# 28 column blocks of an input projection as seven products over both sequences, with other projections between the heads

## The chip, the cores and the metric

The kernel runs on one core of a Trainium2 chip. The metric is the device time of one execution in microseconds (us), as a median of several. TensorE (PE) multiplies matrices, VectorE (DVE), ScalarE (ACT) and GpSimd (POOL) do the elementwise work, and SyncE (SP) issues most of the DMAs.

## The reference

One encoder layer on two sequences of 512 tokens with 1024 channels in float32: a half-step feed-forward block, a mixing block, a second half-step feed-forward block and a last norm.

```
def encoder_layer(x, ...):
    x = x + 0.5 * swiglu(rms_norm(x, ffn1_norm), ffn1_w_gate, ffn1_w_up, ffn1_w_down)
    h = rms_norm(x, mix_norm)
    proj = h @ w_in                                    # 1024 x 4880
    aq, ak, av, mq, mk, mv, gate_pre, o_pre, g_att, g_mlstm = jnp.split(proj, split_at, axis=-1)
    aq = apply_rope(rms_norm(aq.reshape(B, S, 8, 64), q_norm), cos, sin)
    ak = apply_rope(rms_norm(ak.reshape(B, S, 2, 64), k_norm), cos, sin)
    att = gqa_block_attention(aq, ak, av)              # 8 heads of 64, 2 key/value heads
    mem = mlstm_bidirectional(mq, mk, mv, gate_pre, mlstm_gate_bias, o_pre, mlstm_head_norm)   # 4 heads of 128
    merged = jax.nn.sigmoid(g_att) * (att @ w_up_att) + jax.nn.sigmoid(g_mlstm) * (mem @ w_up_mlstm)
    x = x + merged @ w_out
    return x + 0.5 * swiglu(rms_norm(x, ffn2_norm), ffn2_w_gate, ffn2_w_up, ffn2_w_down)
```

In the memory heads each of the two directions needs running maxima of a gate value over the tokens, by which its exponentials are scaled.

## The kernel before

Activations lie with channels on the partitions and 512 tokens along the free axis. A float32 product is made of three matmuls: both operands are split into a high and a low part (`split`, line 658; weights: line 240; one on ACT for the high part, one on DVE for the low), and hi·hi, hi·lo and lo·hi are summed in PSUM.

Five stages follow each other: feed-forward 1 up (0 to 447 us of the span), down (447 to 656), mixing of both sequences (656 to 1431), feed-forward 2 up (1431 to 1854) and down (1854 to 2063), then a tail. In the up stage (class `Up`, matmuls of `product`, line 333) a two by two block product of weights (two column blocks) with tokens (two sequences, two halves of the channels) is made of seven products of sums instead of eight: for each pair of column blocks `gu_left_a/b/c` build and split the sums of weights, and `right_sums` builds those of the tokens once (tiles `xc[B11]`, `xc[B21]`, `xc[B22]`, `xc[T1..T4]`). For ten pairs the first two products, which need sequence 0 alone, are made ahead (`begin`), while the other token sums are still being built; their results wait in DRAM (`kept`).

The mixing stage is a generator `mix(s, ...)`, run for sequence 0 and then 1, the two interleaved at its `yield`s. `tok_proj` (line 739) makes keys, values and gates (272 columns in all), queries (512) and memory values (512) with tokens on the partitions. The other 28 blocks of 128 columns go through `proj_w` (line 755), 24 matmuls of 128x512 each, per sequence: 8 attention gates (`att_gate`), 8 memory gates (`mem_gate`), 4 output gates (`out_gate`), 4 memory queries and 4 memory keys (`mem_qk`). Sequence 0 loads and splits the weights and parks both parts in DRAM (`load_w`, `parked`); sequence 1 loads the parts. These blocks stand in a `queue`, out of which `fill(n)` takes n units after each head, so that PE has something to do while DVE, ACT and POOL work for the head:

```
for h in range(HA):                       # 8 attention heads
    nxt = scores(h + 1) if h + 1 < HA else None
    attend(h, Ps)                         # row maxima, exp, scale, split, transposes, P.V
    ...
    fill(1 if h < 4 else 2)
```

An attention head is: scores (line 1001, 8 matmuls), row maxima (DVE, 1004), exp (ACT, 1006), reciprocal and scaling (1007, 1008), 16 transposes (1020) with a split (658), and P·V (1028, 8 matmuls; drained in 1036 and 1037). Before the heads come the ropes (`rope_apply`, lines 796 to 807), with mean squares (785) and inverse roots in small DVE steps (`rstd_cols`, lines 162 to 192), and transposes to head layout (keys 847, queries 941). A memory head (`mem_head`, `mem_out`) is: scores (1117), exponentials (ACT, 1131), products (1133), merged directions (1144, 1145), transposes (1159) and products with the values (1167); its maxima come out of `mem_max` (POOL add and two DVE reduces, 967 to 973, for each head and direction) and `mem_scales`. `merge_att` and `merge_mem` multiply by the output projections of the two branches and the gates; `out_unit` is one block of the last projection, which for sequence 0 lies around the ropes and heads of sequence 1.

The order of the instructions on each engine is set when the kernel is built: a scheduler takes them by priority, which is the order in the program, moved by `shifted(n)`. On the chip each engine runs its own list in order, and waits for semaphores. Tiles come out of pools with few buffers, so a new tile can wait until an old one was read for the last time.

Of the kernel before, what the change touches and what calls it, by code (L numbers as in the profile page):

```python
# [8 lines left out]
F32 = mybir.dt.float32  # L9
# [7 lines left out]
P = 128  # L17
# [9 lines left out]
def encoder(ctx, tc, I, outs):  # L27
# [679 lines left out]

    held = []

# [12 lines left out]
    def tok_proj(xh, xl, cols, kk, done):  # L722
# [7 lines left out]
        def comp(k0, w):  # L730
            wh, wl = w
            if not p:
                p.extend([MM(), MM(), MM(), PO()])
            for kl in range(kk):
                k = k0 + kl
                for b in range(4):
                    bs = slice(b * P, (b + 1) * P)
                    for i, (a, w_) in enumerate(((xh, wh), (xh, wl), (xl, wh))):
                        nc.tensor.matmul(p[b][:, :N], a[:, k, bs], w_[:, kl, :],  # L739
                                         start=(k == 0 and i == 0), stop=(k == KD - 1 and i == 2))  # L740
            if k0 + kk == KD:
                done(p)

        return [(lambda k0=k0: load(k0), lambda w, k0=k0: comp(k0, w)) for k0 in range(0, KD, kk)]

# [12 lines left out]
    OUT = 3  # L758

    def mix(s, xh, xl, early=None, extra=None, after=None):  # L760

        xsrc = lambda k: (xh[:, k, :], xl[:, k, :])
        queue = []

        def fill(n):
            go(*queue[:n])
            del queue[:n]
# [3 lines left out]

        def win_cols(c0, done):
            return proj(win_v[:, :, c0:c0 + P], ("in", c0), xsrc, KD, done)

# [5 lines left out]
        Gt = small(64, "gt")  # L780
# [32 lines left out]
        def kv_done(pk):  # L813
            for b in range(4):
# [6 lines left out]
                                        op0=ALU.mult, op1=ALU.subtract)  # L821
            ssk = small(8, "ssk")
# [10 lines left out]
        def q_done(pq):  # L833
            ssq = small(32, "ssq")
            for b in range(4):
                t = T2()
                nc.scalar.activation(t, pq[b], AF.Copy, scale=r[s][:, b:b + 1])
# [20 lines left out]
        ebuf = dpool.tile([2, 4, S], F32, name=nm("ebuf"))  # L858

        def gates():  # L860
            Gb = Gt.rearrange("p (b c) -> p b c", b=4)
# [24 lines left out]
            for d in range(2):  # L886
                p = PT()
                for b in range(4):
                    nc.tensor.transpose(p[0:4, b * P:(b + 1) * P], ev[:, d, b, :], ident)
                er = F2()  # L890
                V_.tensor_copy(er[0:4], p[0:4])
                nc.sync.dma_start(ebuf[d], er[0:4])


        Vm = []

        def mem_values():
            def done(pvv):
                vm = A([P, 2, 4, S], F32R, "Vm")
                for b in range(4):  # L900
                    nc.scalar.activation(vm[:, 0, b, :], pvv[b], AF.Copy, scale=r[s][:, b:b + 1])
                    V_.scalar_tensor_tensor(vm[:, 1, b, :], pvv[b], r[s][:, b:b + 1], f(vm[:, 0, b, :]),
                                            op0=ALU.mult, op1=ALU.subtract)
                Vm.append(vm)
            return tok_proj(xh, xl, [(1792, 512)], 2, done)
# [3 lines left out]
        def mem_qk(h, j):  # L909
            def done(pp):  # L910
                if j == 0 and not s:
                    t = wpool.tile([P, 4, S], F32R, tag="w8", bufs=4, name=nm("qk"))
                    qks[h] = [t[:, i] for i in range(4)]
                elif s:
                    t = wpool.tile([P, 2, S], F32R, tag="wr", bufs=4, name=nm("qk"))
                    qks.setdefault(h, []).extend(t[:, i] for i in range(2))
                t = F2()
                V_.tensor_tensor(t, pp, R[s], op=ALU.mult)
                split(t, *qks[h][2 * j:2 * j + 2])
            return win_cols((768, 1280)[j] + h * P, done)  # L920
# [3 lines left out]
        def out_gate(h):  # L924
            def done(pp):
                og = T2(F32, "ac")
                V_.tensor_tensor(og, pp, R[s], op=ALU.mult)
                nc.scalar.activation(og, og, AF.Tanh, scale=0.5)
                G_.tensor_scalar(og, og, 1.0, hn[:, h:h + 1], op0=ALU.add, op1=ALU.mult)
                ogs[h] = og  # L930
            return win_cols(2320 + h * P, done)
# [13 lines left out]
        go(*tok_proj(xh, xl, [(512, 256), (2304, 16)], 2, kv_done))  # L945
        if early:
            early()
        go(*tok_proj(xh, xl, [(0, 512)], 2, q_done), mem_qk(0, 0))
        yield None
# [5 lines left out]
        go(mem_qk(0, 1), mem_qk(1, 0), mem_qk(1, 1))  # L955

        st = spool.tile([P, 4, 2, 4, HM], F32, tag="st", bufs=1, name=nm("st"))
        n1, bd, en, n2 = [st[:, i] for i in range(4)]

        def mem_rows(h, d):  # L960

            eb = T2(F32, "eb")
            nc.sync.dma_start(eb, ebuf[d, h:h + 1, :].rearrange("a s -> (a s)").partition_broadcast(P))
            em = T2(F32, "eb")
            eb3 = eb.rearrange("p (b s) -> p b s", b=4)
# [3 lines left out]

        def mem_max(h, d):  # L970
            eb3, em3 = mem_rows(h, d)
            V_.tensor_reduce(n1[:, d, :, h], em3, axis=AX.X, op=ALU.max)
# [549 lines left out]
```

## Time and profile before

| what | us |
|---|---|
| median of 3 runs (lowest, highest) | 2085.64 (2085.07, 2087.56) |
| the profiled execution's own time | 2083.45 |
| its span | 2081.4 |
| PE, DVE, ACT, POOL busy | 2060.3, 1573.6, 895.4, 111.2 |
| mean granted PE clock | 0.999 |

The profile is one execution. Times in it are from the start of the span. Engines are listed with their busy time; for a group of instructions the page gives line, engine, operation, tiles out<-in, shape and count, then the busy time, the mean duration of one in ns and the idle time of the engine before them with what ended it. The chain is followed back from the last instruction: each piece has its start, its length, and the engine, tile and line.

### The profile page before, as it was taken

The numbers are of one execution on the slowest core, as the hardware profiler recorded it, in microseconds if no ns is written. First come the engines' busy times: TensorE is split into PE (matmuls) and PEld (weight loads), VectorE is DVE, ScalarE is ACT, GpSimd is POOL, SyncE is SP. The second block draws the span as 40 slices with busy tenths as digits, with TensorE's granted clock in tenths as the row PEclk, the third lists the DMA queues.
The fourth block names the chain that finished last, engine by engine and source line by source line (L and its number), as shares of the span: only waits on it lengthen the run. The fifth ranks groups of instructions, "written<-read, shape, count | busy, mean of one in ns | idle before, by whom it ended". The sixth has DMA issues, their size and how long they took to land.

```text
span 2081.4 us, 27314 instructions
## 1 busy us (share of the span) xinstructions
PE 2060.3 (99%) x9488; PEld 1694.0 (81%) x9488; DVE 1573.6 (76%) x2870; ACT 895.4 (43%) x1645; POOL 111.2 (5%) x122
## 2 busy tenths in 40 slices
PE   8999999999999999999999999999999999999998
PEld 6888888888888877888887788888888888888887
DVE  7888888786797899575568846555788888785797
ACT  6544444443234566463344543324444444442222
POOL 1000000001003012100120000002000000000010
PEclk9999999999999999999999999999999999999999
DMA  8656555699766655777685345677656555599753
GB/s 277 208 171 195 193 171 182 201 346 359 260 223 243 216 167 198 257 240 272 214 283 193 112 153 188 208 258 244 200 177 201 193 172 182 187 339 350 273 189 117
DMA packets 303161, 458.52 MB, mean 220 GB/s; under 512 B 20304, under 2 KB 170848, under 8 KB 302000
## 3 DMA queue, kind: packets, MB, share of 16 engines
q1 hardware_dynamic: 301152, 451.32, 64.4%
q0 software_dynamic: 1872, 5.46, 0.8%
q8 instruction: 75, 1.23, 0.2%
q14 instruction: 62, 0.51, 0.1%
HBM read 289.82 MB, written 166.89 MB: 219 GB/s over the span
## 4 chain that ended last, share of the span: by engine, by line
PE 92%; DVE 3%; DMA 3%; ACT 1%; issue 1%; SPq 0%; POOL 0%; DVEq 0%; ACTq 0%; POOLq 0%
PE mm L755 19%; PE pss L333 17%; PE pst L333 11%; PE mm L333 10%; PE mm L589 9%; PE pst L589 4%; PE pss L589 4%; PE mm L739 4%; PE pso L589 3%; PE pso L739 1%; PE pso L1028 1%; PE pso L1167 1%; PE pst L755 1%; PE pss L755 1%; PE pss L1117 1%; PE pst L1020 1%
## 5 line engine op out<-in xcount | busy, mean ns | idle before, releaser
L755 PE MATMUL mm<-xh,w 128*128 128x512 f32 x896 | 290.6, 394 | 0.0
L333 PE MATMUL pss<-xc,w 128*128 128x512 f32 x1056 | 256.4, 392 | 0.2 <-DVE t L364 0.2
L333 PE MATMUL mm<-xc,w 128*128 128x512 f32 x1056 | 253.5, 391 | 2.2 <-ACT w L291 1.4
L333 PE MATMUL pst<-xc,w 128*128 128x512 f32 x1056 | 253.8, 390 | 0.1
L333 PEld LDWEIGHTS pss<-xc,w 128*128 128x128 f32 x1056 | 197.0, 188 | 47.4 <-DVE t L364 6.7
L333 PEld LDWEIGHTS mm<-xc,w 128*128 128x128 f32 x1056 | 197.4, 188 | 45.2 <-ACT w L291 2.3
L333 PEld LDWEIGHTS pst<-xc,w 128*128 128x128 f32 x1056 | 198.2, 188 | 41.6 <-ACT t L368 0.5
L755 PEld LDWEIGHTS mm<-xh,w 128*128 128x128 f32 x896 | 167.4, 188 | 33.6
L589 PE MATMUL mm<-rt,w 128*128 128x512 f32 (+1 forms) x819 | 188.4, 385 | 0.0
L755 PE MATMUL mm<-xl,w 128*128 128x512 f32 x448 | 176.0, 393 | 0.0
L589 PEld LDWEIGHTS mm<-rt,w 128*128 128x128 f32 x819 | 151.4, 188 | 29.8
L291 ACT ACTIVATE w<-t 128x512 fp32r<-128x512 f32 x176 | 106.9, 627 | 138.6 <-issue 55.2
L292 DVE TENSOR_TENSOR w<-t,w 128x512 fp32r<-128x512 f32 x176 | 118.3, 689 | 55.1 <-ACT w L291 53.1
L333 PE MATMUL pss<-xc,f 128*128 128x512 f32 x528 | 126.9, 389 | 0.0
L333 PEld LDWEIGHTS pss<-xc,f 128*128 128x128 f32 x528 | 99.1, 188 | 20.6
L657 ACT ACTIVATE w<-wr 128x512 fp32r<-128x512 f32 x72 | 45.1, 632 | 138.6 <-PE pso L589 70.8
L657 ACT ACTIVATE w<-t 128x512 fp32r<-128x512 f32 x82 | 51.8, 632 | 107.6 <-PE pst L589 62.4
L755 PEld LDWEIGHTS mm<-xl,w 128*128 128x128 f32 x448 | 84.3, 188 | 16.7
L589 PE MATMUL pst<-rt,w 128*128 128x512 f32 x396 | 93.7, 389 | 0.0
L589 PE MATMUL pss<-rt,w 128*128 128x512 f32 x396 | 93.7, 389 | 0.0
L589 PEld LDWEIGHTS pst<-rt,w 128*128 128x128 f32 x396 | 74.3, 188 | 15.4
L589 PEld LDWEIGHTS pss<-rt,w 128*128 128x128 f32 x396 | 74.3, 188 | 15.4
(337 smaller groups left out, 3666.9 us busy)
## 6 DMA issues: line engine op xcount, KB each, us to landing
rt<-rbuf SPq DMA_DIRECT2D x154, 512.0 KB, 5.5
wpark<-w SPq DMA_DIRECT2D x104, 512.0 KB, 3.6
w<-wpark SPq DMA_DIRECT2D x104, 512.0 KB, 4.8
wr<-in_ffn_w_gate_dram SPq DMA_DIRECT2D x62, 512.0 KB, 5.3
rbuf<-tab SPq DMA_DIRECT2D x102, 256.0 KB, 3.8
wr<-in_ffn_w_up_dram SPq DMA_DIRECT2D x44, 512.0 KB, 4.7
rbuf<-f SPq DMA_DIRECT2D x72, 256.0 KB, 3.7
wr<-in_w_in_dram SPq DMA_DIRECT2D x36, 512.0 KB, 5.7
```

The costliest lines, as they stand in the source:

```text
L291: pin(nc.scalar.activation(t[:, 0], src, AF.Copy))
L292: pin(V_.tensor_tensor(t[:, 1], src, f(t[:, 0]), op=ALU.subtract))
L333: nc.tensor.matmul(p, a[:, k, :], xt[:, b, k, :], start=(first and k == 0 and i == 0), stop=(k == HK_ - 1 and i == 2), skip_group_check=True)
L589: nc.tensor.matmul(p, u[:, a, d * P:(d + 1) * P], r[:, b, ts], start=(first and q == 0 and k == 0), stop=(q == len(us) - 1 and k == 2), sk ...
L657: nc.scalar.activation(hi, src, AF.Copy)
L739: nc.tensor.matmul(p[b][:, :N], a[:, k, bs], w_[:, kl, :], start=(k == 0 and i == 0), stop=(k == KD - 1 and i == 2))
L755: nc.tensor.matmul(p, a[:, k, :], b, start=(k == 0 and i == 0), stop=(k == n - 1 and i == 2))
L1020: nc.tensor.transpose(p[:, b * P:(b + 1) * P], Ps[b][:, kb * P:(kb + 1) * P], ident)
L1028: nc.tensor.matmul(po, Vst[:, kv_, hk, :], w, start=(kv_ == 0 and i == 0), stop=(kv_ == 3 and i == 1))
L1117: nc.tensor.matmul(p, qk[a][:, isl], qk[b], start=(n == 0), stop=(n == 2))
L1167: nc.tensor.matmul(po, vm[:, a, t, hs_], b, start=(t == 0 and n == 0), stop=(t == 3 and n == 2))
```

## The change

A new class `Joint` makes the 28 blocks for both sequences at once, as 14 pairs with seven products each, in a stage of its own between feed-forward 1 down and the mixing. Ten pairs are begun ahead with sequence 0's products. Results of gates are passed through tanh, those of memory queries and keys split, and all are stored in DRAM (`jbuf`); `mix` loads them where it needs them. Keys and gates of sequence 1 are made right after sequence 0's projections and parked (`kvpark`); queries and values of sequence 1 are made in halves of 256 columns (`tok_half`) and stand in the queue as fillers for the heads of sequence 0 (`FILLS[0]`); six of the eight output units of sequence 0 are the fillers for the heads of sequence 1 (`FILLS[1]`). The running maxima come from two `tensor_tensor_scan` on a 32x128 tile with the heads on the partitions and two transposes, in place of `mem_max`. The factor `hn` moves from POOL into a product on DVE.

```
+    JP = [(2832 + d * P, 3856 + d * P) for d in range(KD)]
+    JP += [(2320 + 2 * i * P, 2320 + (2 * i + 1) * P) for i in range(2)]
+    JP += [(768 + h * P, 1280 + h * P) for h in range(4)]
+    NJ, RAW, JAHEAD, JLAST = 14, 10, 10, 4
...
+    class Joint:
...
+        def out(self, s, j, u, t):
+            to = jbuf[s][j][u]
+            if j >= RAW:
+                hi = self.ring("h")
+                split(t, hi.bitcast(F32R), t.bitcast(F32R))
+                nc.sync.dma_start(to[:, 0], hi)
+                nc.sync.dma_start(to[:, 1], t)
+            else:
+                nc.scalar.activation(t, t, AF.Tanh, scale=0.5)
+                nc.sync.dma_start(to, t)
+        def first_a(self, W, t):
+            X = MM()
+            product(X, W[B11], self.xc[B11], True)
+            with shifted(SOONER):
+                V_.tensor_tensor(t, X, R[0], op=ALU.mult)
+            return X
...
+        def block(self, j, W, v1, mid):
+            ring, xc = self.ring, self.xc
+            Y, Z = PS(), PT()
+            second = lambda: product(Y, W[T2_], xc[T2_], True)
+            if v1 is not None:
+                second()
+            else:
+                v1 = ring("v")
+                X = self.first_a(W, v1)
+                second()
+                self.first_b(X, W, j, ring("h"))
...
+            product(Z, W[T1], xc[T1], True)
...
+            product(Y, W[T3], xc[T3], False)
...
+            product(Z, W[B22], xc[B22], False)
...
+            product(Y, W[T4], xc[T4], False)
...
+    def tok_half(src, col, half, done):
...
+                for b in range(4):
+                    bs = slice(b * P, (b + 1) * P)
+                    for i, (a, w_) in enumerate(((xh, wh), (xh, wl), (xl, wh))):
+                        nc.tensor.matmul(p[b // 2][:, (b % 2) * HW:(b % 2 + 1) * HW], a[:, bs], w_[:, kl, :], ...)
...
+    FILLS = ((0, 1, 1, 1, 1, 1, 0, 1, 2, 0, 0, 0), (0, 1, 0, 1, 0, 1, 0, 0, 1, 1, 1, 0))
...
-            for d in range(2):
-                p = PT()
-                for b in range(4):
-                    nc.tensor.transpose(p[0:4, b * P:(b + 1) * P], ev[:, d, b, :], ident)
-                er = F2()
-                V_.tensor_copy(er[0:4], p[0:4])
-                nc.sync.dma_start(ebuf[d], er[0:4])
+            p = PT()
+            nc.tensor.transpose(p[0:32, 0:P], et, ident)
+            rows = F2()[0:32]
+            er, run = rows[:, 0:P], rows[:, P:2 * P]
+            V_.tensor_copy(er, p[0:32, 0:P])
+            nc.sync.dma_start(ebuf.rearrange("d b h s -> (d b h) s"), er)
+            V_.tensor_tensor_scan(run[:, ::-1], er[:, ::-1], er[:, ::-1], NEG, op0=ALU.max, op1=ALU.max)
+            V_.tensor_tensor_scan(run[0:16], er[0:16], er[0:16], NEG, op0=ALU.max, op1=ALU.max)
...
-            if h >= 4:
-                mem_max(h - 4, 0)
-                mem_max(h - 4, 1)
-            fill(1 if h < 4 else 2)
+            fill(fills[h])
...
+        load_qk(0)
+        load_og(0)
         for h in range(HM):
+            if h + 1 < HM:
+                load_qk(h + 1)
+                load_og(h + 1)
             Ts = mem_head(h)
-            if h == 0:
-                go(*mem_values())
-            queue.append(merge_att(2 * h))
-            fill(1)
+            fill(fills[HA + h])
+            go(*ups[2 * h:2 * h + 1])
             mem_out(h, Ts)
-            if h + 2 < HM:
-                queue.extend([out_gate(h + 2), mem_qk(h + 2, 0), mem_qk(h + 2, 1)])
-            queue.append(merge_att(2 * h + 1))
-            fill(99)
+            go(*ups[2 * h + 1:2 * h + 2])
+        fill(99)
+        flush()
+        yield None
         mh, ml = A([P, KD, S], F32R, "mh"), A([P, KD, S], F32R, "ml")
-        go(*[mem_gate(d) for d in range(KD)])
         go(*[merge_mem(d) for d in range(KD)])
...
+    jt = Joint(xc)
...
+    jt.rest(raw0)
...
+    m0 = mix(0, src0, None, FILLS[0])
+    next(m0)
+    for d in range(KD):
+        prep1(d)
+    go(*tok_keys_ahead(1, src1))
+    flush()
+    next(m0)
+    for hf in range(2):
+        queue.extend(tok_queries_ahead(1, src1, hf))
+    for hf in range(2):
+        queue.extend(tok_values_ahead(1, src1, hf))
+    next(m0)
...
-    m1 = mix(1, *nhl[1], None, lambda: stats2(0), prep2)
+    OUT = 2
+    m1 = mix(1, None, prep2, FILLS[1])
     next(m1)
     next(m0)
+    outs0, acc0_ = next(m0)
+    go(*outs0[:OUT])
+    queue.extend(outs0[OUT:])
     next(m1)
...
+    outs1, acc1_ = next(m1)
+    go(*outs1)
+    flush()
```

In the main sequence, the first `next(m1)` is where the ropes of sequence 1 stand in the program; the `next(m0)` behind it is `merge_mem` of sequence 0, and the output units come after.

332 lines of the change are left out of this document (238 added, 94 removed).

## The prediction

> **What bounds the kernel now.** I read the page's busy shares and its chain of waits first, then the chain in order of time, then the windows of the stage that is rewritten, and last the groups of that stage's instructions.
>
> ```profile
> span 2081.4 us, 27314 instructions
> PE 2060.3 (99%) x9488; PEld 1694.0 (81%) x9488; DVE 1573.6 (76%) x2870; ACT 895.4 (43%) x1645; POOL 111.2 (5%) x122
> PE 92%; DVE 3%; DMA 3%; ACT 1%; issue 1%; SPq 0%; POOL 0%; DVEq 0%; ACTq 0%; POOLq 0%
> ```
>
> PE is busy for 99% of the span and holds 92% of the chain. PE work that goes is worth its full price, as long as PE still has something to do.
>
> ```profile
> 376.12 2.72 PE pst L333 x12
> 1387.67 43.52 PE mm L755 x192
> 1064.56 0.87 PE pst L941 x8
> 663.22 0.29 PE L739 MATMUL pso<-w,xh 128*128 128x272 f32 x1
> 663.34 0.29 PE L739 MATMUL pso<-w,xl 128*128 128x272 f32 x1
> ```
>
> These rows of the chain and the timeline give PE's prices from start to start (the mean ns of a matmul is its latency, and overlaps its neighbours): a 128x512 matmul 43.52/192 = 0.227 us, and 2.72/12 the same in the feed-forward stage; a 128x128 transpose 0.87/8 = 0.109; a matmul of 272 columns 0.12 to 0.125.
>
> ```profile
> 656.00:1431.00 775.00, 771.50 (x3745) 631.90 (x3744) 513.41 (x1154) 356.86 (x727) 81.83 (x84) 1.00 0.65 215
> 656.00:1431.00 775.00, 517.60 (x2112) 392.83 (x2112) 1.00 0.65 215
> 656.00:1431.00 775.00, 112.99 (x576) 96.15 (x576) 1.00 0.65 215
> ```
>
> Rows of the windows (length, then busy time and count of PE, weight loads, DVE, ACT and POOL, then clock, DMA share, GB/s): the whole mixing stage, and in it the matmuls of line 755 (2112) and of line 739 (576, of which the key-value projections' 192 have 272 columns). By the code the heads add 128 + 128 + 96 + 96 of 512 columns. That is 2944 x 0.2267 + 192 x 0.125 + 609 x 0.109 = 757 us of PE in 775: PE stalls here for only about 18 us. The new order's stalls have to be set against those 18.
>
> **What goes and comes on PE.**
>
> ```profile
> L755 PE MATMUL mm<-xh,w 128*128 128x512 f32 x896 | 290.6, 394 | 0.0
> L755 PE MATMUL mm<-xl,w 128*128 128x512 f32 x448 | 176.0, 393 | 0.0
> ```
>
> These 1344 matmuls are the 28 blocks, 24 matmuls each, for two sequences. In their place stand 14 pairs x 7 products x 12 = 1176: 168 fewer, -38.1 us. Q and V of sequence 1 turn from 192 matmuls of 512 columns into 384 of 256, each between half of 0.227 and the 0.125 of 272 columns: 0 to +4.5, taken +2.5. Sixteen transposes of the gates become six: -1.1. Together -36.7 us, which alone would give 2083.45 - 36.7 = 2046.8.
>
> **What covered the vector work.** The 28 blocks were also the filler between the heads. I go through the new order by place and set PE's content against that of DVE.
>
> ```profile
> 1439.01 0.68 DVE L219 COPY R<-pst 128x512 f32<-128x512 f32 x1
> 1439.61 0.68 DVE L314 TENSOR_TENSOR t<-wr 128x512 f32<-128x512 f32 x1
> L1004 DVE TENSOR_REDUCE asm<-pss 128x1 f32<-128x512 f32 x64 | 43.3, 681 | 1.2 <-PE pss L1001 0.9
> L1008 DVE TENSOR_SCALAR t<-t,asm 128x512 f32<-128x512 f32 x64 | 33.2, 522 | 0.4
> L1007 DVE RECIPROCAL asm<-asm 128x1 f32<-128x1 f32 x64 | 9.7, 156 | 1.4 <-ACT t L1006 1.1
> L658 DVE TENSOR_TENSOR t<-pst,t 128x512 fp32r<-128x512 f32 x96 | 64.7, 686 | 13.5 <-ACT t L657 11.5 <-PE pso L1028 1.3 <-PE pst L1020 0.5
> L1037 DVE TENSOR_TENSOR f<-pso,f 64x512 f32<-64x512 f32 x16 | 11.0, 686 | 5.6 <-ACT f L1036 5.3
> L1001 PE MATMUL pss<-kv,qT 128*128 128x512 f32 x128 | 39.9, 403 | 0.7 <-ACT t L1006 0.7
> L1028 PE MATMUL pso<-t,kv 128*128 128x512 f32 x128 | 47.0, 426 | 0.9 <-ACT t L657 0.7
> L1020 PE MATMUL pst<-ident,t 128*128 128x128 f32 x256 | 39.3, 274 | 1.3 <-DVE t L658 1.1
> 714.00:823.00 109.00, 106.83 (x533) 84.48 (x532) 102.54 (x214) 67.48 (x139) 16.82 (x11) 1.00 0.59 187
> 1104.00:1208.00 104.00, 103.32 (x514) 82.83 (x513) 88.08 (x201) 54.38 (x122) 0.69 (x1) 1.00 0.41 137
> ```
>
> Two DVE instructions of 0.68 start 0.60 apart, so in a full queue each costs 0.08 less than its duration. One of the sixteen attention heads is then, on DVE, four times (0.681 + 0.522 + 0.156 + 0.686), one 0.686 and half a split of 0.686, less 18 x 0.08: 7.6 us. On PE it is 8 + 8 matmuls and 16 transposes: 5.3 us. A head without filler is DVE's by 2.3 us. The last two rows, the two attention parts of before, have PE at 106.8 of 109 and 103.3 of 104, since fillers lay in both.
>
> - **E, attention of sequence 1** (fills 0,1,0,1,0,1,0,0): three output units of 24 matmuls, 5.4 us each, so PE 8 x 5.3 + 3 x 5.4 = 59; DVE 8 x 7.6 and the units' splits, about 64. The stall is 5 if all evens out, and 16 if the five unfilled heads cost 2.3 each and the first and last add 4; taken 10.
> - **B, rope and attention of sequence 0** (0,1,1,1,1,1,0,1): six of eight heads filled, units of 48 half-width matmuls, 5.8 us. Two unfilled heads give 4.6, uneven filling more: 3 to 12, taken 6.
>
> ```profile
> L972 DVE TENSOR_REDUCE st<-box 128x4 f32<-128x512 f32 x16 | 10.8, 677 | 1.0 <-POOL box L967 0.9
> 1306.80:1323.30 16.50, 16.50 (x85) 13.27 (x84) 13.78 (x49) 11.17 (x30) 0.00 (x0) 1.00 0.79 237
> ```
>
> The running maxima help E and B: sixteen such reduces and sixteen like them go, 32 x 0.6 = 19 us of DVE, with their POOL adds; E and B are counted without them. The window is the last memory head of before, 16.5 us with 13.8 of DVE.
>
> - **C and F, memory heads**: by the code a head and its two merging units are 12 + 12 + 24 matmuls and 16 transposes, 12.6 us of PE, where nothing else fills it: three heads of sequence 0, one of sequence 1. Between 13.8 (DVE) and 16.5 (the cycle shown) each loses 1 to 4: 4 to 16, taken 10.
> - **D, the ropes of sequence 1.** Before, they ran while PE had blocks of its own:
>
> ```profile
> 1060.00:1104.00 44.00, 43.67 (x209) 36.28 (x208) 22.54 (x40) 15.03 (x27) 10.24 (x11) 1.00 0.97 329
> 1016.71 0.68 DVE L785 TENSOR_REDUCE ssk<-t 128x8 f32<-128x512 f32 x1
> 1024.46 0.69 DVE L829 TENSOR_TENSOR qT<-t,qT 128x512 fp32r<-128x512 f32 x1
> 1040.16 0.18 DVE L162 TENSOR_SCALAR rs<-ssq 128x32 f32<-128x32 f32 x1
> 1043.09 0.19 DVE L192 SCALAR_TENSOR_TENSOR rs<-rs,rs 128x32 f32<-128x32 f32 x1
> 1059.58 0.68 DVE L796 TENSOR_TENSOR t<-t,rs 128x512 f32<-128x512 f32 x1
> 1062.85 0.68 DVE L796 TENSOR_TENSOR t<-t,rs 128x512 f32<-128x512 f32 x1
> ```
>
> In the new instruction order the 32 transposes of the roped queries stand on PE ahead of all 72 matmuls that project the memory output of sequence 0. Between the last P·V of the memory heads and those 72, PE has 65 small instructions and 7 matmuls, some 8.5 us. DVE has in the same stretch: the key chain, 1016.71 to 1025.15, 8.4; four reduces of the queries, 4 x 0.6 = 2.4; the twelve-step root, 1040.16 to 1043.28 less one foreign 0.6, 2.5; four ropes, 1059.58 to 1062.85 apart, 4 x 3.27 and a last split, 13.5; the twelve-step root of the last memory head, its three large products and splits, the gates and the scales, some 8 by rows of 0.2 and 0.6. Sum 35, so PE waits 26 to 27; queued behind the waiting transposes are those 72 matmuls, whose operands are long there, and then the output units. 20 if DVE comes into this stretch ahead of PE, 31 if it comes late; taken **27**. In this stretch lie also the two scans over 32 rows of 128, which no row shows: between 0.19 (128x32) and 0.68 (a reduce of 512), taken 0.35 each.
>
> ```profile
> 1431.00:1486.00 55.00, 54.81 (x246) 44.99 (x245) 47.69 (x79) 32.70 (x52) 0.56 (x1) 1.00 0.85 269
> L364 DVE TENSOR_TENSOR t<-t,pss 128x512 f32<-128x512 f32 x44 | 30.0, 681 | 0.0
> 656.00:700.00 44.00, 43.84 (x255) 37.90 (x254) 27.42 (x69) 25.89 (x45) 12.60 (x17) 1.00 0.86 290
> ```
>
> - **J, the joint stage** begins like the second feed-forward stage (first row: 20 products ahead, DVE 47.7 of 55, no stall), but its 20 drains lie on DVE, 20 x 0.6 = 12 more: 60 against 55, stall 5, and 1 for the rest; 0 to 10, taken 6.
> - **A, keys, queries, values and the keys of sequence 1**: 68 us of PE by the prices above, in which 20 to 25 MB move. The last row moved 290 GB/s beside a PE that did not stall; at the 329 of the row in D, 25 MB take 76 us. 0 to 8, taken 2.
> - **G, merging of sequence 1 and its output units**: DVE 31 against PE 31 with little between them: 0 to 5, taken 3.
> - At nothing: the stored gates and qk blocks are read back several heads before use; hn moves from POOL into a DVE product that is there anyway.
>
> Sum of the stalls: 10 + 6 + 10 + 27 + 6 + 2 + 3 = 64, ends 32 and 98 (all low, all high at once), a likely 45 to 85. Against the 18 of before: +46. The change: -36.7 + 46 = +9.3 us, so 2092.8 by the profiled execution's time. That execution is 2.2 below the median of the runs shown, 2085.64, so the forecast is **2095.0**.
>
> **Rivals.**
>
> *The stall D is hidden.* If the memory heads of sequence 0 leave DVE idle often enough to do keys, roots and ropes early, D shrinks; from D = 18 down the change is faster. At D = 5 the time is 2095 - 22 = 2073, and with low ends elsewhere less. For it: memory heads with fillers are PE's. Against it: the new order has these DVE instructions behind the last memory head's, and an engine takes them in that order. Chance 0.2.
>
> *The clock falls in the gaps.*
>
> ```profile
> 2063.00:2075.00 12.00, 9.42 (x78) 8.76 (x76) 10.51 (x43) 6.41 (x25) 0.00 (x0) 1.00 0.37 138
> 2075.00:2082.00 7.00, 0.00 (x0) 0.00 (x0) 2.16 (x9) 1.33 (x2) 0.00 (x0) 0.54 0.54 204
> ```
>
> The granted clock is 0.54 where PE does nothing for 7 us, and 1.00 in the 12 us before, with gaps and mostly transposes. If the seven unfilled attention heads ran at half clock, each would take 10.6 on PE in place of DVE's 7.6: 7 x 3 = 21, and 2 more behind D: 2118. Against it speaks the first row. Chance 0.07. The Trainium skill, "TensorE: Matmul & The Clock Gate", Part 1, has half clock after one idle window of some 3.4 us, which the second row bears out, and in Part 4 says that transposes do not count as busy in the same way; by that, D with its 48 transposes would leave the clock at half. The first row, 1.00 over 12 us of mostly transposes, does not show that.
>
> *Vector and transfers stall the joint stage and A at their high ends*, 10 + 8 and the heads at theirs: +20, 2115. For it: DMA at 0.85 to 0.97. Chance 0.1.
>
> *Half-width matmuls cost as much as full ones*: 384 x 0.11 = +42, 2137. The 272-column rows speak against it. Chance 0.03.
>
> **The numbers.** The forecast's own case, stalls of 45 to 85, gives 2076 to 2116 and has 0.6. The range 2072 to 2120 takes in D hidden down to 4 us, the clock and the transfers, and leaves out under 0.2. 0.2% is 4.2 us, about what a measurement of this kernel can tell from no change; within it lie stalls of 50 to 59, a fifth of the main case (0.12), and a little of the first rival (0.01). Faster are the rest of the first rival (0.19) and the main case below 50 (0.03): 0.22; same 0.13; slower 0.65.
>
> **What would show it.** Right: PE's matmuls about as many as before, 36.7 us less at their prices; a stretch of 25 to 30 us between the last memory head of sequence 0 and its merging with PE at a quarter and DVE full; attention of sequence 1 with DVE busier than PE. Wrong: that stretch short or absent, or PE at 97% and more of the mixing stage; a granted clock under 1.00 inside it; a joint stage of well over its 1176 x 0.2267 = 267 us.

## The result and the profile after

The changed kernel takes 2166.2 us as a median of 4 runs (2162.6 to 2167.8), the kernel before 2086.6 (2085.1 to 2087.6): 1.038 of before, 95% interval 1.036 to 1.040. Forecast were 2095, a range up to 2120. The sign was right, the size was not: +80 us in place of +9. The page of the profiled execution after (span, busy shares, the granted clock in 40 slices, the chain):

```profile
span 2163.6 us, 27752 instructions
PE 2070.3 (96%) x9502; PEld 1691.9 (78%) x9502; DVE 1677.2 (78%) x3043; ACT 944.9 (44%) x1744; POOL 93.1 (4%) x106
PEclk9999999999999999999999698999999999999999
PE 84%; DVE 8%; DMA 3%; ACT 3%; issue 1%; POOL 0%; SPq 0%; DVEq 0%; ACTq 0%; POOLq 0%
```

PE's share of the chain fell from 92% to 84%, and there is a slice in which the clock is 6 tenths. The windows of the changed kernel show where (length, busy time and count of PE, weight loads, DVE, ACT and POOL, then clock, DMA share, GB/s). In order: the first part of the joint stage and its rest; attention and memory heads of sequence 0; the stretch of the ropes and the merging behind them; attention and memory heads of sequence 1.

```profile
656.00:740.00 84.00, 76.18 (x325) 60.38 (x324) 74.49 (x121) 37.37 (x56) 8.57 (x6) 0.98 0.69 211
740.00:939.00 199.00, 199.00 (x881) 164.74 (x880) 133.18 (x205) 74.77 (x124) 0.00 (x0) 1.00 0.55 171
1042.00:1104.00 62.00, 56.65 (x339) 46.24 (x337) 50.43 (x107) 41.48 (x95) 2.57 (x2) 0.97 0.34 108
1104.00:1190.00 86.00, 79.34 (x428) 64.82 (x426) 67.65 (x193) 54.37 (x133) 10.33 (x6) 0.96 0.62 206
1190.00:1240.00 50.00, 28.05 (x110) 22.09 (x110) 38.71 (x116) 19.21 (x36) 3.48 (x3) 0.62 0.27 88
1240.00:1265.00 25.00, 25.00 (x114) 19.77 (x113) 22.75 (x36) 11.88 (x23) 8.46 (x5) 1.00 0.90 319
1265.00:1348.00 83.00, 67.72 (x312) 48.55 (x310) 61.96 (x126) 44.42 (x99) 5.52 (x6) 0.92 0.19 63
1348.00:1441.00 93.00, 80.74 (x348) 59.64 (x346) 61.69 (x190) 48.87 (x124) 6.10 (x7) 0.91 0.68 223
```

The ropes' 50 us have PE at 28 and the clock at 0.62. But attention and memory heads of sequence 1 are poor too: PE at 68 of 83 and 81 of 93, while DVE is at 62 in both. Neither engine is full there. The view of waits, from 1014 to 1510 us (engine and line that wait, what ended the wait, us in total, times, longest), names what PE waited for:

```profile
PE pst L1152 <- DVE t L658: 13.9, 4, 9.3
PE pss L1206 <- ACT t L1211: 13.9, 9, 4.4
PE pss L1306 <- DVE t L1322: 5.8, 6, 1.9
PE pst L1225 <- DVE t L658: 5.2, 8, 1.7
```

The first is the rope transposes, as forecast. The second, scores (1206) waiting for exponentials (1211), is in no step of the prediction.

The table sets, place by place, the forecast stall against the measured one: the length of the place less its PE instructions at the prices of the prediction (0.1195 us for half-width matmuls, as measured), summed over the trace. "Waits" are the part of it in which PE stood idle ahead of an instruction, beyond the price of the one before; the rest is PE running slowly.

| place (us of the span) | forecast | measured | of it waits |
|---|---|---|---|
| J joint stage, 656 to 939 | 6 | 11.5 | 9.0 |
| A projections, 939 to 1014 | 2 | 1.6 | 0.6 |
| B ropes and attention, sequence 0, to 1104 | 6 | 15.6 | 8.6 |
| C memory heads, sequence 0, to 1189.5 | } 10 | 14.4 | 7.6 |
| F memory heads, sequence 1, 1348 to 1441 | } | 25.4 | 14.2 |
| D ropes of sequence 1, merging, to 1265 | 27 | 34.6 | 24.4 |
| E attention, sequence 1, to 1348 | 10 | 27.3 | 18.9 |
| G merging and output, sequence 1, to 1510 | 3 | 5.4 | 3.1 |
| sum | 64 | 136 | 86 |

PE's work at these prices fell by 37.0 us (36.7 forecast), and 136 - 18 - 37 = 81 is the loss: the spans differ by 82.2. So the miss lies in the stalls alone. One sign of the prediction didn't come: in attention of sequence 1 DVE isn't busier than PE (62.0 against 67.7 us), and PE's instructions there are worth only 56 us at the prices.

### The profile page after: what moved, and what is told of

Same layout as the page of the kernel before. It is cut to its first block, busy times and chain, and to the rows that moved or that the text cites. A ratio compares the mean times of both kernels' runs of the same rounds, so it can differ in the third digit from the quotient of the medians.

```text
span 2163.6 us, 27752 instructions
## 1 busy us (share of the span) xinstructions
PE 2070.3 (96%) x9502; PEld 1691.9 (78%) x9502; DVE 1677.2 (78%) x3043; ACT 944.9 (44%) x1744; POOL 93.1 (4%) x106
## 4 chain that ended last, share of the span: by engine, by line
PE 84%; DVE 8%; DMA 3%; ACT 3%; issue 1%; POOL 0%; SPq 0%; DVEq 0%; ACTq 0%; POOLq 0%
PE pss L333 22%; PE pst L333 14%; PE mm L333 11%; PE mm L589 8%; PE mm L915 5%; PE pst L589 4%; PE pss L589 4%; PE pso L589 2%; PE mm L867 2%; PE mm L898 2%; PE pss L1206 1%; PE pst L1225 1%; PE pso L1233 1%; PE pso L1356 1%; PE pss L915 1%
## 5 line engine op out<-in xcount | busy, mean ns | idle before, releaser
L333 PE MATMUL mm<-xc,w 128*128 128x512 f32 x1392 | 334.8, 392 | 6.9 <-DVE f L752 2.5
L333 PE MATMUL pss<-xc,w 128*128 128x512 f32 x1392 | 337.3, 391 | 0.2 <-DVE t L364 0.2
L333 PE MATMUL pst<-xc,w 128*128 128x512 f32 x1392 | 334.7, 389 | 0.0
L333 PEld LDWEIGHTS mm<-xc,w 128*128 128x128 f32 x1392 | 261.0, 189 | 65.4 <-DVE w L292 4.3
L333 PEld LDWEIGHTS pss<-xc,w 128*128 128x128 f32 x1392 | 259.8, 188 | 60.8 <-DVE t L364 6.8
L333 PEld LDWEIGHTS pst<-xc,w 128*128 128x128 f32 x1392 | 261.3, 188 | 54.3
L292 DVE TENSOR_TENSOR w<-wr,w 128x1024 fp32r<-128x1024 f32 x58 | 72.7, 1257 | 28.4 <-ACT w L291 28.4
L915 PE MATMUL mm<-mh,w 128*128 128x512 f32 x256 | 85.2, 406 | 1.9 <-ACT w L239 1.3
L291 ACT ACTIVATE w<-wr 128x1024 fp32r<-128x1024 f32 x58 | 61.2, 1056 | 52.2 <-PE pst L333 21.6
L658 DVE TENSOR_TENSOR t<-pst,t 128x512 fp32r<-128x512 f32 x96 | 64.8, 688 | 22.6 <-ACT t L657 19.2
```

Source lines behind the costliest of these rows:

```text
L291: pin(nc.scalar.activation(t[:, 0], src, AF.Copy))
L292: pin(V_.tensor_tensor(t[:, 1], src, f(t[:, 0]), op=ALU.subtract))
L333: nc.tensor.matmul(p, a[:, k, :], xt[:, b, k, :], start=(first and k == 0 and i == 0), stop=(k == HK_ - 1 and i == 2), skip_group_check=True)
L658: (eng or V_).tensor_tensor(lo, src, f(hi), op=ALU.subtract)
L915: nc.tensor.matmul(p, a[:, k, :], b, start=(k == 0 and i == 0), stop=(k == n - 1 and i == 2))
```

## The experiments

All times are medians; ratios are to runs of the kernel before on the same chip. That kernel took 2084.0 to 2086.6 us on the chips used, so a difference between medians of two experiments carries some 2 us. The edits are against the changed kernel unless said otherwise.

**e1: merging ahead of the ropes.** This takes away the order in the queue that D was explained by.

```
     m1 = mix(1, None, prep2, FILLS[1])
-    next(m1)
     next(m0)
     outs0, acc0_ = next(m0)
     go(*outs0[:OUT])
+    next(m1)
     queue.extend(outs0[OUT:])
```

> One edit to the changed kernel: the merging of sequence 0's memory output and its first two output units stand in the program ahead of the ropes of sequence 1, no longer behind them. Theory (the ropes of sequence 1 stand on PE ahead of matmuls that are ready, D): the 50 us between the last memory head of sequence 0 and its merging, with PE waiting for 24 us and at half clock for 10, shrink to under 15; the output units then cover the ropes, so some of them are gone as fillers from the heads of sequence 1, which cost there up to 10; total 2166 - 34 + 10, about 2140. Rival (the stretch is bound by DVE work that has to be done anyway, and is only moved): under 8 us gained, 2158 or more.

2169.3 us, 1.041 (1.040 to 1.043): nothing gained, the rival's result. The stretch from the last memory head to the first score-heavy part of attention, in this kernel:

```profile
1189.00:1275.00 86.00, 69.67 (x304) 52.38 (x302) 70.33 (x166) 35.64 (x70) 11.29 (x7) 0.90 0.47 167
```

PE now does its merging and four of the eight output units in this stretch, and waits for the rope transposes for 6.8 us in place of 13.9. But the first head of attention is done no sooner, at 1274.8 us against 1272.5: DVE has 70 of 86 us to do, before the edit 71 in the same window. So the order on PE was not what cost; what is left as the cause is DVE's amount of work between the two attentions, which e9 tests.

**e2: useless matmuls in the unfilled heads of sequence 1.**

```
             fill(fills[h])
+            if s and not fills[h]:
+                idle = MM()
+                for _ in range(10):
+                    nc.tensor.matmul(idle, qT[:, h, 0:P], kv[:, (h // 4) * 2, :], start=True, stop=True)
```

> The changed kernel with ten useless 128x512 matmuls (2.3 us) added at each of the five attention heads of sequence 1 that have no filler; they feed nothing, and nothing else is changed. Theory (the granted clock falls in the gaps and slows what PE does next): the windows of 3.4 us with a clock near 0.5 in attention of sequence 1 become fewer, and its 83 us fall by 3 to 9; total 2157 to 2163. Rival 1 (the heads are held by the chain through DVE and ACT alone, and PE has room): time unchanged within 2 us, whatever the clock. Rival 2 (PE has no room, the gaps are short): up to 5 x 2.3 = 11 us longer.

2164.8 us (2163.2 to 2168.4), the same as without: 50 matmuls, 11 us of PE, cost nothing. The granted clock from 1265 to 1348 us rose from 0.92 to 0.96. PE has that much room in E, and warming it so lightly brings nothing: rival 1.

**e3: the running maxima alone, in the kernel before.** The edit is the scans and transposes of the change's diff, without the rest.

> The kernel before with the running maxima alone: two scans over 32 x 128 and transposes in place of a row maximum per head and direction; the column blocks stay as they were. Theory (the maxima's DVE work lay beside a busy PE): 19 us of DVE and 16 POOL adds go, PE stays at 99%, the time falls by 0 to 4 us: 2083 to 2087. Rival (DVE was late in places of attention): 5 to 10 us less.

2082.2 against 2084.0 us, ratio 0.9991 (0.9982 to 1.0001): at most 2 us, as the theory had it. DVE's busy time on that page is 1550.5 us (1573.6 before) and PE's 2060.2. The maxima by themselves, beside a busy PE, slow nothing down.

**e4: finer fillers.** e1's edit, output units in halves of 12 matmuls, one to each head of sequence 1, and query and value units of 24 half-width matmuls.

```
-    FILLS = ((0, 1, 1, 1, 1, 1, 0, 1, 2, 0, 0, 0), (0, 1, 0, 1, 0, 1, 0, 0, 1, 1, 1, 0))
+    FILLS = ((1, 1, 1, 1, 1, 1, 1, 1, 2, 2, 2, 2), (1, 1, 1, 1, 1, 1, 1, 1, 1, 1, 1, 1))
...
+            return [(load, lambda _: comp(0)), (lambda: None, lambda _: comp(1))]
```

> The first edit (merging ahead of the ropes) and finer fillers: the output units in halves of 12 matmuls, one to each of the twelve heads of sequence 1, and the query and value units of sequence 1 in halves of 24 half-width matmuls, one to each attention head and two to each memory head of sequence 0. Theory (stalls come from heads without filler, and the clock falls in their gaps): attention of both sequences and the memory heads lose half of their stalls, some 30 us, and with the merging 25 more: about 2110. Rival (the heads are held by their own chain through DVE and ACT and not by a lack of matmuls): no better than the merging edit alone, about 2140.

2170.1 us, 1.041: the theory that a little PE work in each head would do falls. But each unit brought its drain along, as in the changed kernel: PE's waits for exponentials are still 13.3 us (13.9). The next run changes that drain alone.

**e5: the square of an output unit from another pool.** In the timeline of the changed kernel (start, length, engine, line, in brackets the idle time before it and its end) a filled head of sequence 1 ends like this:

```profile
1323.86 0.68 DVE L1209 TENSOR_REDUCE asm<-pss 128x1 f32<-128x512 f32 x1
1327.80 0.59 ACT L1241 ACTIVATE f<-pso 64x512 f32<-64x512 f32 x1 [1.31 <-PE pso L1233]
1328.42 0.69 DVE L1242 TENSOR_TENSOR f<-pso,f 64x512 f32<-64x512 f32 x1 [1.21 <-ACT f L1241]
1329.15 0.63 ACT L657 ACTIVATE att<-f 128x512 fp32r<-128x512 f32 x1 [0.76 <-DVE f L1242]
1329.81 0.69 DVE L658 TENSOR_TENSOR att<-f,att 128x512 fp32r<-128x512 f32 x1 [0.70 <-ACT att L657]
1330.54 0.69 DVE L1396 SCALAR_TENSOR_TENSOR f<-mm,f 128x512 f32<-128x512 f32 x1
1331.26 0.63 ACT L155 ACTIVATE t<-f 128x512 f32<-128x512 f32 x1 [1.48 <-DVE f L1396]
1331.80 0.67 ACT L1211 ACTIVATE t<-pss,asm 128x512 f32<-128x512 f32 x1
1332.61 1.89 PE L1206 MATMUL pss<-kv,qT 128*128 128x512 f32 x4 [4.41 <-ACT t L1211]
```

Rows in between are left out. The last two row maxima of the next scores are there at 1322.9 and 1324.5; their exponentials run at 1331.8 and 1332.5. On ACT they stand behind the square of the output unit (line 155), which waits for the unit's sum on DVE (1396), which stands behind the split of the head's output (658), which waits for ACT. The scores of the head after that wait for the PSUM bank that an exponential reads. The square takes its tile from the pool of eleven, out of which the exponentials' tiles come as well, ahead of them in the program.

```
-                acc[0] = sq_add(xt, acc[0], "R", "t2", V_ if d == KD - 1 else None)
+                acc[0] = sq_add(xt, acc[0], "R", "t2" if s else "f2", V_ if d == KD - 1 else None)
```

> The changed kernel with one edit: the square of an output unit of sequence 0 (line 155) takes its buffer from the pool of four and no longer from the pool of eleven out of which the heads' exponentials and transposed rows come. Theory (a filler holds up the head behind it, since its square stands on ACT ahead of exponentials that are ready, and waits there for a sum on DVE that comes late): in the instruction order the square comes behind the exponentials; the three gaps of 4.2 to 4.4 us on PE ahead of line 1206 go, attention of sequence 1 falls from 83 us by 8 to 13, total 2153 to 2158. Rival (the unfilled heads are held by DVE's 7.6 us each): under 3 us gained.

2151.5 us, 1.0315 (1.030 to 1.033): 14.7 less. The square now stands behind the exponentials in ACT's list. PE's waits for exponentials in attention of sequence 1, of the changed kernel and of this one:

```profile
PE pss L1206 <- ACT t L1211: 10.9, 5, 4.4
```

```profile
PE pss L1206 <- ACT t L1211: 1.0, 2, 0.7
```

From the last P·V matmul of its first head to that of its last, attention of sequence 1 takes 62.1 us and no longer 75.5. The theory holds.

The same measure head by head shows where the time was. In the changed kernel a head with no filler ahead of it takes 7.2 to 8.1 us, one behind a filler 15.3, 16.4 and 17.0 (the last head, whose scores are done by then, 3.7). With the square moved, heads without take 7.5 to 8.2, and those behind a filler 11.9, 11.7 and 11.1.

**e6: the weights' low parts on POOL**, to take 20 us from DVE.

```
-            hi, lo = split_w(raw, V_)
+            hi, lo = split_w(raw, G_ if key[0] in ("up", "out") else V_)
```

> The changed kernel with the low parts of the weights of both up-projections and of the last projection (sequence 0, 16 instructions of 128x1024, 1.25 us each on DVE) made on POOL, which is busy for 4% of the span. Theory (from the end of attention of sequence 0 on, DVE sets the pace and PE waits for it): the 20 us taken from DVE shorten the stretch from the first memory head to attention of sequence 1 by 8 to 18; total 2148 to 2158. Rival (the pace is that of the chain through PE, ACT and DVE in one head, and the splits lie in its gaps): under 4 us either way.

2185.0 us, 1.047: 19 us slower, which neither had. Two rows of its timeline show what happens, and then DVE's groups from 1104 to 1200 us, of this kernel and of the changed one:

```profile
1163.56 2.36 POOL L240 TENSOR_TENSOR w<-wr,w 128x1024 fp32r<-128x1024 f32 x1
1164.28 5.44 DVE L1334 SCALAR_TENSOR_TENSOR t<-t,dn,t 128x128 f32<-128x128 f32 x3
L1334 DVE SCALAR_TENSOR_TENSOR t<-t,dn,t 128x128 f32<-128x128 f32 x16 | 13.3, 866 | 0.0
L658 DVE TENSOR_TENSOR mem<-box,mem 128x512 fp32r<-128x512 f32 x3 | 4.6, 1539 | 0.0
L1322 DVE SCALAR_TENSOR_TENSOR t<-pss,t 128x512 f32<-128x512 f32 x8 | 5.5, 690 | 1.3 <-ACT t L1320 1.3
```

```profile
L1334 DVE SCALAR_TENSOR_TENSOR t<-t,dn,t 128x128 f32<-128x128 f32 x16 | 6.4, 407 | 0.0
L658 DVE TENSOR_TENSOR mem<-box,mem 128x512 fp32r<-128x512 f32 x3 | 2.0, 682 | 0.0
L1322 DVE SCALAR_TENSOR_TENSOR t<-pss,t 128x512 f32<-128x512 f32 x8 | 5.5, 690 | 1.5 <-ACT t L1320 1.3
```

These products of SBUF tiles (line 1334) take twice as long on average: in this trace the ten that ran beside a POOL instruction took 1.74 us each, the 22 others 0.34. PE's waits for them in the memory heads grow from 3.7 to 7.2 us, and 3.6 come up for the splits behind them; the rest of the 19 us was not traced wait by wait. DVE's load as such isn't tested by this run.

**e7: 64 us of useless matmuls.** 20 at each of the eleven unfilled heads of both sequences, 16 ahead of each query rope of sequence 1.

```
+    def useless(n, a, b):
+        p = MM()
+        for _ in range(n):
+            nc.tensor.matmul(p, a, b, start=True, stop=True)
...
         for b in range(4):
+            if s:
+                useless(16, Vms[1][:, 0, 0, 0:P], Vms[1][:, 0, 1, :])
             q_rope(b)
```

> The changed kernel with 284 useless 128x512 matmuls (64 us at 0.227) that feed nothing: 20 at each unfilled head of attention (seven) and of memory (four), and 16 ahead of each of the four query ropes of sequence 1. Theory (PE stands idle there for the sake of DVE and ACT, and the lost work was only cover): most of the 64 us vanish in the gaps, the time grows by 0 to 20, and the granted clock of the mixing stage goes up. If the low clock itself cost much, the time falls below 2160. Rival (PE is still what bounds the heads): 2166 + 64 = 2230.

2175.6 us, 1.043: 64 us of PE work cost 9.4. The stretch from attention of sequence 0 to the end of the memory heads of sequence 1, in the changed kernel and in this one:

```profile
1014.00:1442.00 428.00, 364.53 (x1829) 285.16 (x1829) 327.87 (x831) 240.69 (x554) 38.15 (x38) 0.91 0.47 156
```

```profile
1014.00:1442.00 428.00, 405.55 (x2122) 326.99 (x2122) 327.13 (x831) 241.74 (x554) 36.90 (x38) 0.97 0.47 156
```

The last P·V of the memory heads comes at 1441.2 and 1441.8: up to there some 264 useless matmuls, 60 us, cost 0.6 in the execution that was profiled, the fastest of the four (2171.3 us). So PE's amount of work is not what bounds this stretch, and cover of this kind was nearly free. That is a net result, since the clock went from 0.91 to 0.97 as well. Attention of sequence 1 became 6.5 us shorter (1272.0 to 1341.0 from its first head's last P·V to its last head's, before 1272.5 to 1348.0) although it had useless work at five heads and the squares still stood ahead of the exponentials: the one place where the low clock can be seen to cost time. The other parts became longer by about as much.

**e8: four edits together** (e1, e5, e6, and two of the four query ropes of sequence 1 on POOL).

> Four edits together: merging ahead of the ropes, the square in the other pool, the weights' low parts on POOL, and two of the four query ropes of sequence 1 on POOL. Theory (DVE's queue sets the pace between the two attentions, and a filler's square holds up heads behind it): the stretch of 160 us from the last memory head of sequence 0 to the end of attention of sequence 1 falls by 30 to 45, total 2120 to 2135. Rival (latency of the chain in each head): 2150 or more. In neither case does it come down to the 2084 of the kernel before.

2179.7 us, 1.045. After e6 this is no surprise: if the effects add up, the two POOL edits give back more than the other two bring. The total is the rival's, but not for the rival's reason. It says nothing on e1 with e5 alone, which wasn't run.

**e9: without the query ropes of sequence 1.**

```
-            qo = rope_apply(qraw[b], rq[0][:, b * 8:(b + 1) * 8], tabs[0], b).rearrange(...)
+            qo = (qraw[b] if s else rope_apply(qraw[b], rq[0][:, b * 8:(b + 1) * 8], tabs[0], b)).rearrange(...)
```

> The changed kernel without the four query ropes of sequence 1: the raw queries are split and transposed as they are, so normalisation and rotation of those queries are left out (some 11 to 13 us of DVE; the small root chain stays). Theory (in the stretch D PE waits for DVE's ropes): the 50 us stretch after the last memory head of sequence 0 falls by 9 to 14, and the total with it, to 2152 to 2157. Rival (the stretch waits for loads or for the merging): under 4 us.

2152.7 us, 1.032: 13.5 less, for 11 to 13 us of DVE work. The first head of attention of sequence 1 ends its P·V at 1258 and no longer at 1272. D is DVE's time, nearly one for one.

**e10: the fillers of sequence 1 all in attention, on top of e5.**

```
-    FILLS = ((0, 1, 1, 1, 1, 1, 0, 1, 2, 0, 0, 0), (0, 1, 0, 1, 0, 1, 0, 0, 1, 1, 1, 0))
+    FILLS = ((0, 1, 1, 1, 1, 1, 0, 1, 2, 0, 0, 0), (1, 1, 1, 0, 1, 1, 1, 0, 0, 0, 0, 0))
```

> The kernel of the moved square (2151.5 us) with the six output units that serve as fillers all in attention of sequence 1 (fills 1,1,1,0,1,1,1,0) and none in its memory heads. Theory (a filler in a memory head holds the head up by its drain, as in attention, since the last memory head, without one, takes 16.6 us and the filled ones 25; attention has PE room since useless matmuls vanished in it): memory heads of sequence 1 fall by 15 to 25, attention grows by 5 to 12; total 2135 to 2145. Rival (the units cost their 5.4 us of PE wherever they stand): 2150, within 4.

2130.8 us, 1.0215 (1.020 to 1.023): 20.7 less than e5 and 35 less than the change, and below the theory's 2135 to 2145. Its windows of attention and memory heads of sequence 1:

```profile
1265.00:1344.00 79.00, 77.49 (x392) 60.93 (x392) 71.08 (x146) 54.34 (x122) 11.35 (x12) 1.00 0.56 190
1344.00:1410.00 66.00, 60.10 (x294) 45.45 (x292) 52.96 (x177) 39.99 (x104) 0.56 (x1) 1.00 0.64 202
```

Against 83 and 93 us in the changed kernel: attention is now PE's (77 of 79), and the clock is 1.00 in both. From the end of attention to the first memory head's last P·V it takes 16.7 us, and from there from P·V to P·V 18.4, 18.3 and 15.5 (e5: 23.8, 25.3, 24.7, 16.6); attention takes 65.5 (e5: 62.1). So three units cost some 21 us beside the memory heads, and 3.4 beside attention, against 16 us of PE work. Which step of a unit holds the memory heads up was not taken apart.

**e11: the 20 early drains of the joint stage on ACT.**

```
-                V_.tensor_tensor(t, X, R[0], op=ALU.mult)
+                if ahead:
+                    nc.scalar.activation(t, X, AF.Copy)
+                else:
+                    V_.tensor_tensor(t, X, R[0], op=ALU.mult)
...
```

The scaling by the inverse root of sequence 0 is left out of those blocks.

> The changed kernel with the 20 drains of the joint stage's begun blocks on ACT as plain copies; the scaling by the root of sequence 0 is left out of those blocks. Theory (at the start of the joint stage DVE is late by its drains): the 11.7 us that PE loses in the stage fall by 3 to 6; total 2160 to 2163. Rival (what PE loses there are waits for the statistics and the token sums): under 2 us.

2160.4 us, 1.035, 5.8 less, at the theory's upper end (its four runs spread over 8 us, 2153.9 to 2161.8). The waits for those drains are gone from the stage, and it ends at 933.5 us and no longer at 939.9; a wait of 2.5 us for the statistics of sequence 1 stays.

**e12: the values of sequence 1 moved to the ropes, on top of e10.**

```
-    FILLS = ((0, 1, 1, 1, 1, 1, 0, 1, 2, 0, 0, 0), (0, 1, 0, 1, 0, 1, 0, 0, 1, 1, 1, 0))
+    FILLS = ((0, 1, 0, 1, 0, 1, 0, 1, 0, 0, 0, 0), (1, 1, 1, 0, 1, 1, 1, 0, 0, 0, 0, 0))
...
-    for hf in range(2):
-        queue.extend(tok_values_ahead(1, src1, hf))
...
     m1 = mix(1, None, prep2, FILLS[1])
+    go(*tok_values(1, src1))
+    flush()
     next(m1)
```

> The kernel of the placed fillers (2130.8 us) with the memory values of sequence 1 as full-width matmuls (96 of 512 columns, 21.8 us) between the memory heads and the ropes of sequence 1, no longer as eight-head fillers of sequence 0; the heads of attention of sequence 0 keep the four query units (fills 0,1,0,1,0,1,0,1,0,0,0,0). Theory (PE work is worth nothing where it has room and its time where it covers DVE: attention and memory heads of sequence 0 have PE room, and the ropes have no cover): the values' 23 us of PE leave the heads of sequence 0, whose length falls by 5 to 15, and part of them vanishes under the ropes, whose PE waits of 25 us fall to 10 to 18; total 2110 to 2124. Rival (the heads of sequence 0 are as long as their DVE and ACT chain whether filled or not, and the ropes wait for the same chain): 2128 or more.

2123.9 us, 1.019 (1.017 to 1.021): 6.9 less, at the theory's upper edge. The memory heads of sequence 0 end at 1173.8 and no longer at 1190.6, so PE work left them. But of the values' 96 matmuls 45 still ran in those heads and the others right behind them, up to 1186 us. The ropes' transposes, from 1211 us on, stayed bare, and that half of the theory failed:

```profile
PE pst L1152 <- DVE t L658: 13.3, 4, 8.7
```

This is the best of the versions run, and still 39 us behind the kernel before.

## Why the prediction missed

**Right: PE's work.** -36.7 forecast, -37.0 in the trace. The half-width matmuls cost 0.119 to 0.12 each, in the middle of the bounds. In the chain of the changed kernel:

```profile
1021.50 2.14 PE mm L898 x18
1024.51 2.99 PE mm L898 x25
```

So the rival of a full price for half-width matmuls is out.

**Near in size, half right in cause: D.** 27 forecast, at most 31; 34.6 measured, 24.4 of it waits. The rope transposes do wait for DVE, and the matmuls behind them too (the first wait of the list above). But the step "72 matmuls that are ready stand behind them" isn't what costs: with those put first (e1) attention begins no sooner and nothing is gained, and with 11 to 13 us of DVE work taken away (e9) 13.5 us go. The rival that hid D had little to stand on.

**Wrong: the price of a head with a filler.** The step that failed set each head at the larger of its DVE and PE totals, and so put a head with a filler at its PE work, with no stall: 5.3 + 5.4 = 10.7 us in attention of sequence 1, 12.6 + 5.4 = 18.0 in its memory heads. Stalls were counted for unfilled heads alone, 10 us in E and 10 in all memory heads. That is a price for full queues. Measured were 27 and 40. The unfilled heads of sequence 1 came out as forecast: 7.2 to 8.1 us in attention (7.6 forecast; the terms given for it add up to 7.8), 16.3 for the last memory head (13.8 to 16.5). The filled ones took 15.3 to 17.0 and 24.8 to 26.4, some 17 us more than forecast over three heads of attention and some 23 over three memory heads (the first of these counted from the end of attention). Two things made up most of it. An output unit is a filler with a drain of its own: load, sum on DVE, square on ACT, add on POOL. The blocks that it replaced had one or two steps, and no square. Its square held up ready exponentials (e5, 14.7 us). And units in memory heads cost more than their 5.4 us of PE, some 7 each, in attention with the square moved about 1 (e10, 20.7 us); why memory heads bear them so badly stays open. Together 35 of the 72 us by which the stalls exceeded the forecast. That "DVE is later than PE by 2.3 us in an unfilled head" was right; that a filler mends it held only once its square was out of the way: e4 put fillers in every head with the squares where they were and gained nothing.

**Too low a chance: the clock.** It had 0.07 and +23 us. The row that was held against it, 12 us at 1.00, was misread as mostly transposes with gaps: at least 48 of its 78 PE instructions are matmuls of 256 columns, and PE was full for its first 6.8 us. Half of the rival came true: from 656 to 1510 us of the changed kernel the granted clock fell to a half thirteen times. Rows of 3.4 us of the changed kernel, in D (not all of them):

```profile
1211.20:1214.60 3.40, 0.00 (x0) 0.00 (x0) 2.98 (x11) 0.59 (x2) 0.00 (x0) 0.87 0.00 0
1214.60:1218.00 3.40, 0.00 (x0) 0.00 (x0) 3.21 (x8) 0.00 (x0) 0.00 (x0) 0.50 0.00 0
1218.00:1221.40 3.40, 1.94 (x8) 1.57 (x8) 3.37 (x9) 1.52 (x4) 0.00 (x0) 0.50 0.00 0
1224.80:1228.20 3.40, 1.94 (x8) 1.57 (x8) 3.25 (x8) 1.72 (x5) 0.00 (x0) 0.50 0.80 211
1235.00:1238.40 3.40, 3.40 (x17) 2.82 (x16) 2.64 (x4) 2.30 (x3) 0.61 (x1) 1.00 0.22 88
```

PE idle, then 0.50 while eight transposes a window run, then 1.00 once PE is full. This agrees with the Trainium skill, "TensorE: Matmul & The Clock Gate", Part 1 (half clock after one idle window of about 3.4 us, full after one busy one). In this trace a window need not be wholly idle, though: in the 3.4 us ahead of the thirteen falls PE was busy for 0.00 to 1.73 us. By Part 4 of that page of the Trainium skill transposes don't count as busy in the same way. D alone can't show that, since PE was also idle for 1.5 us of each such window, and the start of the same execution speaks against it for these float32 transposes: PE does 3.4 us of them and nothing else, without a gap, at half clock, and then has the full clock.

```profile
12.20:15.60 3.40, 3.40 (x18) 3.37 (x17) 1.35 (x7) 3.40 (x8) 0.23 (x1) 0.50 1.07 300
15.60:19.00 3.40, 2.69 (x18) 1.67 (x16) 3.40 (x6) 3.23 (x8) 0.00 (x0) 1.00 1.08 348
```

Of the 136 us of stall some 36 at most are PE running slowly at a low clock (50 us are not waits, and before 14 of the 18 weren't either). Waits that a slow PE made longer are not in that figure. In e7, with the clock at 0.97 and 60 us more work, the stretch was as long, so a faster PE and more work for it may cancel there. What the clock alone cost the end time is left open; the 6.5 us that attention lost in e7 are the one sign of its size.

**Mis-sized: J and B.** 11.5 for 6: the early drains were half of it (e11), the rest waits for statistics and weight splits. B was 15.6 for 6. Its attention takes some 62 us with 128 half-width matmuls in it (changed kernel) and with 70 (e12): those heads too go at a pace that isn't PE's, in e12 7.6 to 8.8 us without a filler and 11.2 to 11.7 with one. The rival of transfers that stall PE has little for it: A lost 1.6 us of a possible 8, and PE's waits for DMA from 656 to 1510 us come to 1.0.

**The whole.** The sign came from comparing a gain in PE's work with the loss of cover, and that held. No version run here won the cover back: of the loss of 80 us some 40 can be had back by other places for the fillers and another pool (e12); of what is left the largest pieces are D, where DVE has its ropes and PE has little to lay beside them, and attention of sequence 0, 26 and 23 us in e12 by the measure of the table.

## What to carry to other kernels

Matmuls saved in a kernel that PE bounds are worth their price only where PE stays the bound; here 168 matmuls fewer (38 us) took 1344 away from under DVE and ACT chains that had been hidden, and the chains came out. Before gathering PE work into a stage of its own, price every stage that it leaves by the chain through all engines and not by each engine's total, the filled places as well as the bare ones; a run with useless matmuls in the gaps shows how much PE room there is, net of what they do to the clock. A filler is judged by its drain as well: which engine's list its last step stands in, from which pool it takes its tile, and who is behind it.

## What the hardware showed

DVE and POOL got in each other's way more than any step had it (e6): three DVE products of 128x128, 1.2 us at the mean of 407 ns in the changed kernel, took 5.44 beside POOL's 2.36, and the split of the memory output went from 682 to 1539 ns on average. DVE products that read PSUM (line 1322) stayed at 690 ns. The Trainium skill, "SBUF — State Buffer", "SBUF: two separate sides", says that DVE and GpSimd share one port pair as an exclusive lock, held for the whole instruction; these rows agree. A scan over 32 x 128 takes 404 ns, within the bounds of the prediction.

```profile
L1116 DVE TENSOR_TENSOR_SCAN f<-f 32x128 f32<-32x128 f32 x2 | 0.8, 404 | 0.0
```
